# The state chain of a hybrid decoder layer with its per-head products on 128x64 tiles

## The chip, the cores and the metric

The kernel runs on one core of one Trainium2 chip. The metric is device microseconds of one execution. The core has five engines that work beside each other: PE (TensorE, the matrix engine), ACT (ScalarE), DVE (VectorE), POOL (GpSimd) and SP (SyncE, which here only issues DMAs). Each runs its own list of instructions in the order in which the program lists them and waits on semaphores for the others. A matmul reads a stationary operand, which a separate weight load (PEld in the profile) puts into the array, and a moving operand whose columns stream through it.

## The reference, cut to what matters

One layer: RMSNorm, one input projection, a pooling mixer (A) beside RWKV-7 time mixing (B), an output projection, then an MLP. The change lies in (B), in the scan over 1024 prompt tokens with 8 heads of 64:

```python
def step(S, inp):
    r_t, w_t, k_t, v_t, aa_t, bb_t = inp
    sa = jnp.einsum('bhvk,bhk->bhv', S, aa_t)
    S = S * w_t[:, :, None, :] + sa[..., None] * bb_t[:, :, None, :] + v_t[..., None] * k_t[:, :, None, :]
    return S, jnp.einsum('bhvk,bhk->bhv', S, r_t)
S_final, y = lax.scan(step, S0.astype(f32), xs)
```

## The kernel before, in words

The 1024 prompt tokens are cut into chunks of 64, and the scan is done chunk by chunk: within a chunk by matrices, from chunk to chunk by a 64x64 state per head. Heads go in pairs (`hp`, four pairs), tokens in two halves of 512, so there are eight units (`Unit`), each with 8 chunks. Partitions 0 to 63 hold head 0 of the pair, 64 to 127 head 1 (`R[0]`, `R[1]`).

For a unit, `rkv` projects r, k, v; `stage1` makes per chunk the operands `AR`, `RB`, `BKT` and `SV`; `inverse` makes `TT`, the inverse of a triangular matrix, block by block for both heads; `chain` (line 578) then runs the 8 chunks one after the other, each a step. For head h, the slice `SV[:, c, h, :]` holds the state in the head's own 64 partitions and the chunk's values in the other 64. So each product contracts over all 128 partitions. Before the change a product handles both heads at once: pq (line 601) is `AR` times `SV` for all 128 rows and both heads' 128 columns, and only the two diagonal 64x64 blocks are read on. A step is:

- `sg`: ACT scales the state (line 596)
- pq and the first part of py, the outputs (lines 601, 602): PE, stationary `AR` and `SV`
- `Q`: ACT copies pq out of PSUM (line 604)
- pa (line 605): PE, `TT` times `Q`; ACT copies its two diagonal blocks into `SV`, in place of the state (line 607)
- pu and the second part of py (lines 608, 609): PE, stationary `BKT` and `SV`
- two DVE instructions (line 617) write the new state, one per head, into the next chunk's `SV` (or into `Sf` at a unit's end)

After every four steps `ys` copies the outputs out of PSUM and `post` (line 626) normalises them. All these products are plain fp32: a 128x128 one goes through PE as two passes, each with its own weight load and its own matmul record, so the 64 executions of a line leave 128 records.

The other products of PE at that time (projections `pj`, line 185 in the helper `gemm`, the scores `sc` of line 431, transposes of lines 445 and 449, and late in the stage the output projection `mx`) are mostly 128x128 too. They stand between the chain's products. The order is not written out by hand: the parts are emitted in the sequence of `ORDER` (line 42), `chain` at a raised priority (`lead_chain`, line 824), and a scheduler that knows dependencies and its own costs lays out each engine's list when the program is built. What it lays out is fixed; at run time PE goes through its list in order. After the chain stage come the output projection, the MLP's up products (line 1014) and down products (`dn`, line 185).

Three places use smaller tiles of the array before the change: `lora_up` (line 352, 64 rows, 128 columns), the `inverse` (lines 548, 555, 565, 570: 32x32 tiles) and `decode` (line 705: 128 rows, 64 columns).

Of the kernel before, what the change touches and what calls it, by code (L numbers as in the profile page):

```python
# [7 lines left out]
F32 = mybir.dt.float32  # L8
F32R = mybir.dt.float32r
AF = mybir.ActivationFunctionType  # L10
ALU = mybir.AluOpType
# [4 lines left out]
P = 128  # L16
# [24 lines left out]
QUEUE = 1  # L41
ORDER = """R0 S0 R1 I0 S1 Q C0 R2 S2 I1 C1 R3 S3 I2 P00 P01 T I3 P02 L R4 C2 S4 C3 R5 S5 I4 R6 C4 S6 I5 R7 C5 S7 I6 C6 P10 I7 P11 P12 D"""
NBV = 3
# [43 lines left out]
def _build(ctx, nc, tc, I, O, dbg):  # L87
    V, A, PE, SY, GP = nc.vector, nc.scalar, nc.tensor, nc.sync, nc.gpsimd
# [4 lines left out]
    def act(out, in_, func=AF.Copy, bias=0.0, scale=1.0, **k):  # L93
        A.activation(out, in_, func, bias=bias, scale=scale, **k)  # L94

    def open_pool(stack, name, bufs=1, **k):
        return stack.enter_context(tc.tile_pool(name=name, bufs=bufs, **k))

    R = (slice(0, 64), slice(64, 128))
# [91 lines left out]
    rcp = open_pool(st_left, "rcp", reuse_waits="tile")  # L191
    ps_c = open_pool(st_left, "psc", 1, space=PSUM)
    pcs = ps_c.tile([P, 512], F32, name="pcs")
# [137 lines left out]
    def low_rank(half):  # L331
        n = HALF[half][1]
        z0 = big(f"z0{half}", "f")
        zw, za = (zp.tile([P, 520], F32R, tag=x, name=f"{x}{half}") for x in ("zw", "za"))
        z1 = zp.tile([P, 520], F32, tag="z1", name=f"z1{half}", bufs=2)
        shifted(12, half, z0)
        shifted(13, half, z1)
        if half:
            project_later()
        sigm(z0[0:64, :n], z0[0:64, :n], 0.0, 2.0)  # L340
        V.tensor_scalar(z0[0:64, :n], z0[0:64, :n], -2.0, 1.0, ALU.mult, ALU.add)
        for z, r, q in ((zw, R[0], R[1]), (za, R[1], R[0])):
            act(z[r, :n], z0[r, :n])
            V.tensor_tensor(z[q, :n], z0[r, :n], f32(z[r, :n]), op=ALU.subtract)
        sigm(z1[:, :n], z1[:, :n], 0.0, -1.0)
        Zt[half] = (zw, za, z1)
# [231 lines left out]
    def chain(U):  # L578
        hp = U.hp
        z1 = Zt[U.half][2]  # L580
        for i in range(2):
            nm = f"{hp}_{2 * U.half + i}"
            AR, RB, BKT, SV, TT = U.AR[i], U.RB[i], U.BKT[i], U.SV[i], U.TT
            if i == 0:
                for h in range(2):
                    if U.half == 0:
                        GP.memset(SV[R[h], 0, h, :], 0.0)
                    else:
                        act(SV[R[h], 0, h, :], Sf[hp][R[h], :])
            pyp = ps_y.tile([P, 512], F32, tag="y", name=f"py{nm}")  # L590
            py = pyp.rearrange("p (c h t) -> p c h t", h=2, t=64)
            for c in range(4):
                g = 4 * i + c
                gn = f"{U.nm}_{g}"
                sg = rcp.tile([P, 2, 64], F32, tag="sg", name=f"sg{gn}", bufs=2)
                act(sg, SV[:, c, :, :], scale=U.gam[:, g:g + 1])

                o = 256 * (hp % 2)
                pq, pa = (pcs[:, o + 128 * q:o + 128 * q + 128].rearrange("p (h t) -> p h t", t=64) for q in range(2))
                pu = pq  # L600
                PE.matmul(pq, AR[:, c, 0, :, :], SV[:, c, :, :], start=True, stop=True)  # L601
                PE.matmul(py[:, c, :, :], SV[:, c, :, :], AR[:, c, 1, :, :], start=True, stop=False)
                Q = rcp.tile([P, 2, 64], F32, tag="Q", name=f"Q{gn}", bufs=2)
                act(Q, pq)
                PE.matmul(pa, TT[:, g, :, :], Q, start=True, stop=True)  # L605
                for h in range(2):
                    act(SV[R[h], c, h, :], pa[R[h], h, :])
                PE.matmul(pu, BKT[:, c, :, :], SV[:, c, :, :], start=True, stop=True)  # L608
                PE.matmul(py[:, c, :, :], SV[:, c, :, :], RB[:, c, :, :], start=False, stop=True)
                for h in range(2):  # L610
                    if g == 7:
                        dst = Sf[hp][R[h], :]
                    elif c == 3:
                        dst = U.SV[1][R[h], 0, h, :]
                    else:
                        dst = SV[R[h], c + 1, h, :]
                    V.scalar_tensor_tensor(dst, pu[R[h], h, :], U.gam[R[h], g:g + 1], sg[R[h], h, :], ALU.mult, ALU.add)
            ys = rcp.tile([P, 256], F32, tag="ys", name=f"ys{nm}", bufs=2)
            for h in range(2):
                act(ys[R[h]].rearrange("p (c t) -> p c t", t=64), py[R[h], :, h, :])  # L620
            post(hp, nm, pyp, ys, 256, U.bv[:, 256 * i:256 * i + 256], z1[:, 256 * i:256 * i + 256], ys)
            QM.dma_start(mix_d[4 + hp][U.half][:, 256 * i:256 * i + 256], ys)
        if U.half:
            QM.dma_start(O["wkv_p"][hp], Sf[hp])

    def post(hp, nm, ps, ys, n, bv, zg, out):

        pm, pv = ps[:, 256:512], ps[:, 0:256]
        PE.matmul(pm[:, :n], CJ, ys, start=True, stop=True)
        q = rcp.tile([P, 256], F32, tag="q", name=f"q{nm}", bufs=1)  # L630
        act(q[:, :n], pm[:, :n], AF.Square)
        PE.matmul(pv[:, :n], BO, q[:, :n], start=True, stop=True)
        act(q[:, :n], pv[:, :n], AF.Ln, bias=EPSG, scale=1.0 / 64)
        act(q[:, :n], q[:, :n], AF.Exp, scale=-0.5)
        V.tensor_tensor(out, pm[:, :n], q[:, :n], op=ALU.mult)
        V.scalar_tensor_tensor(out, out, col(V_LG, hp), bv, ALU.mult, ALU.add)
        pg = pm
        PE.matmul(pg[:, :n], glu[:, hp * P:(hp + 1) * P], zg, start=True, stop=True)
        V.scalar_tensor_tensor(out, out, col(V_LB, hp), pg[:, :n], ALU.add, ALU.mult)
# [184 lines left out]
    def lead_chain(U):  # L824
        with tc.high_priority(offset=LEAD):
            chain(U)
# [18 lines left out]
    for c in ORDER.split():  # L845
# [4 lines left out]
        else:  # L850
            {"Q": pool_rows, "T": later_tokens, "L": lambda: low_rank(1), "D": decode_start}[c]()
    dec = dec[0]
# [287 lines left out]
    for b in (1, 2):  # L1140
        c, n = BLK[b]
# [88 lines left out]
```

## Time and profile before

| | |
|---|---|
| time, median of 3 runs | 1336.7 us (1336.37 to 1336.93) |
| the profiled execution's own time | 1335.81 us |
| its span, first to last instruction | 1334.0 us |
| mean granted TensorE clock | 0.991 of full speed |
| chain stage, first to last step | 67 to 521 us of the span |

PE busy is the time covered by its matmul records, whose ends are modelled and which overlap: a pass starts before the one in front has ended. So the steps from one start to the next are what a stream of passes costs, and the rows are read by starts. A row of the timeline gives the start, the length, engine, line, operation, tiles, the tile of the array (rows*columns), shapes and a count of equal instructions merged into it.

### The profile page before, as it was taken

The page shows a single profiled execution, that of the slowest core. Times are in us where ns is not written, and L with a number is a line of the kernel's source. Part 1 is how long each engine was busy: PE and PEld are TensorE (multiplying, and loading weights), DVE is VectorE, ACT ScalarE, POOL GpSimd, SP SyncE. Part 2 cuts the span into 40 slices and gives each one's busy share as a digit, 9 for nine tenths or more (in the row PEclk, how much of TensorE's full clock was granted, in tenths as well). Part 3 has the DMA queues.
Part 4 walks back from the last instruction along what each step waited for, and adds up shares of the span by engine and source line. Part 5 has one row for each costly group of instructions (what it writes and reads, how often), then busy time and mean ns, then how long its engine had stood idle before and what let it go on. Part 6 is the DMA issues. An engine that isn't in the chain of part 4 may idle for free.

```text
span 1334.0 us, 27179 instructions
## 1 busy us (share of the span) xinstructions
PE 1267.3 (95%) x10230; PEld 1146.4 (86%) x10230; DVE 1050.9 (79%) x2331; ACT 822.5 (62%) x2015; POOL 125.4 (9%) x248
## 2 busy tenths in 40 slices
PE   5999999899999989989999999999899999999996
PEld 5987788798777867789989888998799999999996
DVE  8897687778877756589989997786698787878775
ACT  7668677776777657364757564555465645455552
POOL 4101001210011021110002320001000000000000
PEclk9999999999999989999999999999899999999999
DMA  6323123222222253442335663335634323332321
GB/s 209 102 54 83 43 50 90 95 93 53 66 56 48 63 164 135 142 149 80 119 115 150 181 167 96 113 97 186 217 99 147 103 89 105 94 106 93 104 71 64
DMA packets 119492, 143.19 MB, mean 107 GB/s; under 512 B 55769, under 2 KB 71257, under 8 KB 119353
## 3 DMA queue, kind: packets, MB, share of 16 engines
q1 hardware_dynamic: 97184, 92.22, 23.7%
q0 software_dynamic: 20320, 47.39, 11.4%
q10 hardware_dynamic: 1856, 1.85, 0.4%
q8 instruction: 80, 1.31, 0.4%
q14 instruction: 52, 0.42, 0.1%
HBM read 120.68 MB, written 20.97 MB: 106 GB/s over the span
## 4 chain that ended last, share of the span: by engine, by line
PE 68%; ACT 12%; DVE 11%; DMA 5%; issue 4%; POOL 1%; SPq 0%; DVEq 0%; ACTq 0%; POOLq 0%
PE dn L185 23%; PE b L1014 21%; PE pj L185 8%; PE mx L185 4%; ACT SV L94 2%; DMA a<-in_w_up 2%; PE pcs L608 1%; PE sc L431 1%; ACT wh L94 1%; ACT TT L94 1%; PE pcs L605 1%; DVE tm L525 1%; PE pcs L601 1%; DVE wl L167 1%; PE bkt L445 1%
## 5 line engine op out<-in xcount | busy, mean ns | idle before, releaser
L185 PE MATMUL dn<-uh,wh 128*128 128x260 f32 (+1 forms) x736 | 237.7, 324 | 6.1 <-DVE x L1080 4.3
L185 PE MATMUL dn<-ul,wh 128*128 128x260 f32 (+1 forms) x736 | 237.4, 323 | 1.2 <-DVE ul L1025 1.2
L185 PE MATMUL dn<-uh,wl 128*128 128x260 f32 (+1 forms) x736 | 237.2, 323 | 1.0 <-DVE wl L167 1.0
L94 ACT ACTIVATE wh<-a 128x512 fp32r<-128x512 f32 x192 | 120.8, 629 | 161.3 <-PE dn L185 85.0
L94 ACT ACTIVATE wh<-wr 128x512 fp32r<-128x512 f32 x230 | 142.9, 622 | 98.6 <-PE dn L185 26.0
L185 PE MATMUL pj<-xh,wh 128*128 128x258 f32 (+3 forms) x576 | 172.3, 299 | 13.7 <-ACT wh L94 13.7
L167 DVE TENSOR_TENSOR wl<-wr,wh 128x512 fp32r<-128x512 f32 x230 | 155.7, 681 | 35.4 <-ACT wh L94 27.5
L185 PE MATMUL pj<-xl,wh 128*128 128x258 f32 (+3 forms) x576 | 170.3, 296 | 0.0
L185 PE MATMUL pj<-xh,wl 128*128 128x258 f32 (+3 forms) x576 | 170.0, 295 | 0.1
L185 PEld LDWEIGHTS dn<-uh,wh 128*128 128x128 f32 x736 | 138.9, 189 | 17.3 <-ACT uh L94 3.2
L185 PEld LDWEIGHTS dn<-uh,wl 128*128 128x128 f32 x736 | 138.8, 189 | 12.3 <-DVE wl L167 1.2
L185 PEld LDWEIGHTS dn<-ul,wh 128*128 128x128 f32 x736 | 138.9, 189 | 10.8 <-DVE ul L1025 1.8
L176 DVE TENSOR_TENSOR wl<-a,wh 128x512 fp32r<-128x512 f32 x192 | 131.3, 684 | 6.2 <-ACT wh L94 3.6
L1080 DVE TENSOR_TENSOR x<-dn,x 128x260 f32<-128x260 f32 (+1 forms) x192 | 97.6, 511 | 41.5 <-PE dn L185 39.9
L185 PEld LDWEIGHTS pj<-xh,wh 128*128 128x128 f32 x576 | 109.9, 191 | 17.6 <-ACT wh L94 13.7
L185 PEld LDWEIGHTS pj<-xl,wh 128*128 128x128 f32 x576 | 110.0, 191 | 2.3 <-issue 1.9
L185 PEld LDWEIGHTS pj<-xh,wl 128*128 128x128 f32 x576 | 109.8, 191 | 1.8 <-issue 1.0
L94 ACT ACTIVATE c<-c 128x256 f32<-128x256 f32 (+1 forms) x128 | 53.1, 415 | 45.7 <-DVE c L1029 45.2
L991 DVE TENSOR_TENSOR a<-a,a 128x512 f32<-128x512 f32 x96 | 66.2, 689 | 19.0 <-DMA a<-in_w_up 17.5
L1025 DVE TENSOR_TENSOR ul<-u,uh 128x256 fp32r<-128x256 f32 (+1 forms) x128 | 53.6, 423 | 18.8 <-ACT uh L94 18.4
L185 PE MATMUL mx<-mh,wh 128*128 128x260 f32 (+1 forms) x192 | 64.9, 341 | 3.3 <-ACT mh L94 1.9
L185 PE MATMUL mx<-ml,wh 128*128 128x260 f32 (+1 forms) x192 | 63.6, 332 | 0.9 <-DVE ml L881 0.9
(421 smaller groups left out, 3388.6 us busy)
## 6 DMA issues: line engine op xcount, KB each, us to landing
a<-in_w_up SPq DMA_DIRECT2D x128, 256.0 KB, 2.6
wr<-in_w_down SPq DMA_DIRECT2D x128, 256.0 KB, 2.6
wr<-in_w_in POOLq DMA_DIRECT2D x72, 256.0 KB, 3.1
wr<-in_w_out POOLq DMA_DIRECT2D x26, 256.0 KB, 3.2
xr<-in_xT SPq DMA_DIRECT2D x16, 256.0 KB, 3.6
mr<-mix SPq DMA_DIRECT2D x8, 260.0 KB, 4.3
x<-in_xT SPq DMA_DIRECT2D x4, 520.0 KB, 5.0
blk<-AA SPq DMA_DIRECT2D x16, 128.0 KB, 2.7
```

Of the source, the lines that this page charges most:

```text
L94: A.activation(out, in_, func, bias=bias, scale=scale, **k)
L167: V.tensor_tensor(l[:, :w], raw[:, :w], f32(h[:, :w]), op=ALU.subtract)
L176: V.tensor_tensor(l, raw, f32(h), op=ALU.subtract)
L185: PE.matmul(ps, lhs, rhs, start=i == 0, stop=i == n - 1)
L431: PE.matmul(psc[:, c, :], BK[:, c, 2 * h:2 * h + 2, :], AR[:, c, :, h, :], start=True, stop=True)
L445: PE.transpose(pt[:, c, :], BK[:, c, 2 * h:2 * h + 2, :].rearrange("p a t -> p (a t)"), ident)
L525: V.tensor_tensor(pr[:, q], l[:, q].unsqueeze(2).to_broadcast([64, m, m, m]), r[:, q].rearrange("p k j -> p j k").unsqueeze(1).to_broadcas ...
L601: PE.matmul(pq, AR[:, c, 0, :, :], SV[:, c, :, :], start=True, stop=True)
L991: V.tensor_tensor(a[out], a[x], a[y], op=op)
L1014: PE.matmul(ps, lhs[:, c], rhs, start=k == i == 0, stop=k == 3 and i == 2)
L1025: V.tensor_tensor(ul, u, f32(uh), op=ALU.subtract)
L1080: V.tensor_tensor(d, ps[:, :n], d, op=ALU.add)
```

## The change

The two heads' products are issued one by one. Each keeps the contraction over 128 partitions, but loads 64 columns of weights and moves 64 columns, on the half of the array's columns that belongs to the head (tile position 0 or 64), so that its result lands in the head's 64 partitions of PSUM. Only the diagonal blocks are computed. pq, pa, pu, `Q` and `ys` become compact: 64 columns instead of 2x64. `pa` stays one product with the block-diagonal `TT` on the whole array, with 64 moved columns. pu gets its own place in PSUM instead of pq's. `ys` is one ACT copy instead of two.

```diff
--- before.py
+++ after.py
@@ -588,7 +588,7 @@
                     else:
                         act(SV[R[h], 0, h, :], Sf[hp][R[h], :])
             pyp = ps_y.tile([P, 512], F32, tag="y", name=f"py{nm}")
-            py = pyp.rearrange("p (c h t) -> p c h t", h=2, t=64)
+            py = pyp[:, 0:256].rearrange("p (c t) -> p c t", t=64)
             for c in range(4):
                 g = 4 * i + c
                 gn = f"{U.nm}_{g}"
@@ -596,17 +596,20 @@
                 act(sg, SV[:, c, :, :], scale=U.gam[:, g:g + 1])
 
                 o = 256 * (hp % 2)
-                pq, pa = (pcs[:, o + 128 * q:o + 128 * q + 128].rearrange("p (h t) -> p h t", t=64) for q in range(2))
-                pu = pq
-                PE.matmul(pq, AR[:, c, 0, :, :], SV[:, c, :, :], start=True, stop=True)
-                PE.matmul(py[:, c, :, :], SV[:, c, :, :], AR[:, c, 1, :, :], start=True, stop=False)
-                Q = rcp.tile([P, 2, 64], F32, tag="Q", name=f"Q{gn}", bufs=2)
+                pq, pa, pu = (pcs[:, o + 64 * q:o + 64 * q + 64] for q in range(3))
+                for h in range(2):
+                    PE.matmul(pq[R[h]], AR[:, c, 0, h, :], SV[:, c, h, :], start=True, stop=True)
+                for h in range(2):
+                    PE.matmul(py[R[h], c, :], SV[:, c, h, :], AR[:, c, 1, h, :], start=True, stop=False)
+                Q = rcp.tile([P, 64], F32, tag="Q", name=f"Q{gn}", bufs=2)
                 act(Q, pq)
                 PE.matmul(pa, TT[:, g, :, :], Q, start=True, stop=True)
                 for h in range(2):
-                    act(SV[R[h], c, h, :], pa[R[h], h, :])
-                PE.matmul(pu, BKT[:, c, :, :], SV[:, c, :, :], start=True, stop=True)
-                PE.matmul(py[:, c, :, :], SV[:, c, :, :], RB[:, c, :, :], start=False, stop=True)
+                    act(SV[R[h], c, h, :], pa[R[h]])
+                for h in range(2):
+                    PE.matmul(pu[R[h]], BKT[:, c, h, :], SV[:, c, h, :], start=True, stop=True)
+                for h in range(2):
+                    PE.matmul(py[R[h], c, :], SV[:, c, h, :], RB[:, c, h, :], start=False, stop=True)
                 for h in range(2):
                     if g == 7:
                         dst = Sf[hp][R[h], :]
@@ -614,10 +617,9 @@
                         dst = U.SV[1][R[h], 0, h, :]
                     else:
                         dst = SV[R[h], c + 1, h, :]
-                    V.scalar_tensor_tensor(dst, pu[R[h], h, :], U.gam[R[h], g:g + 1], sg[R[h], h, :], ALU.mult, ALU.add)
+                    V.scalar_tensor_tensor(dst, pu[R[h]], U.gam[R[h], g:g + 1], sg[R[h], h, :], ALU.mult, ALU.add)
             ys = rcp.tile([P, 256], F32, tag="ys", name=f"ys{nm}", bufs=2)
-            for h in range(2):
-                act(ys[R[h]].rearrange("p (c t) -> p c t", t=64), py[R[h], :, h, :])
+            act(ys, pyp[:, 0:256])
             post(hp, nm, pyp, ys, 256, U.bv[:, 256 * i:256 * i + 256], z1[:, 256 * i:256 * i + 256], ys)
             QM.dma_start(mix_d[4 + hp][U.half][:, 256 * i:256 * i + 256], ys)
         if U.half:
```

On PE, the list of the program before at the second and third step of a unit (`sc`, `bkt`, `vt`, `pj` belong to other units; L608 and L609 end a step, L601 and L602 begin the next, L605 is pa):

```order
L608 MATMUL pcs<-SV_0_1223,BKT_0_1222 128x128
L609 MATMUL py_0_1922<-RB_143,SV_0_1223 128x128
L445 MATMUL bkt_0_1_1716<-cst,BK 128x128 x4
L449 MATMUL vt_0_1722<-cst,v_0_1433 128x128 x2
L601 MATMUL pcs<-SV_0_1223,AR_139 128x128
L602 MATMUL py_0_1922<-AR_139,SV_0_1223 128x128
L185 MATMUL pj_1_2170<-xh_205,wh 128x258
L185 MATMUL pj_1_2170<-xl_206,wh 128x258
L605 MATMUL pcs<-Q_0_1_1940,TT_158 128x128
```

The same unit in the changed program, from the end of its second step to the third's pa (L610 is pu, L612 and L603 are py, L601 is pq, L606 is pa; 64x64 is one head's product):

```order
L610 MATMUL pcs<-SV_0_1223,BKT_0_1222 64x64 x2
L612 MATMUL py_0_1952<-RB_143,SV_0_1223 64x64 x2
L431 MATMUL sc_1_1_1775<-AR_138,BK 128x128
L185 MATMUL pj_0_2271<-xh_171,wl 128x256
...
L445 MATMUL bkt_1_0_1785<-cst,BK 128x128 x2
L603 MATMUL py_0_1952<-AR_139,SV_0_1223 64x64
L445 MATMUL bkt_1_0_1785<-cst,BK 128x128 x2
L601 MATMUL pcs<-SV_0_1223,AR_139 64x64 x2
L603 MATMUL py_0_1952<-AR_139,SV_0_1223 64x64
L185 MATMUL pj_0_2271<-xh_171,wl 128x256
```

The first head's py product now stands by itself among whole-array products, ahead of the two pq products: it needs only the first of the two DVE instructions that write the state.

And the end of the fourth step of that unit in the changed program, PE again:

```order
L606 MATMUL pcs<-Q_0_3_2010,TT_158 128x64
L185 MATMUL pj_1_2300<-xl_206,wh 128x258
L185 MATMUL pj_1_2300<-xh_205,wl 128x258
L185 MATMUL pj_1_2300<-xh_205,wh 128x258
L612 MATMUL py_0_1952<-RB_143,SV_0_1223 64x64
L610 MATMUL pcs<-SV_0_1223,BKT_0_1222 64x64 x2
L612 MATMUL py_0_1952<-RB_143,SV_0_1223 64x64
L185 MATMUL pj_1_2300<-xl_206,wh 128x258
```

Here one head's second py product moved ahead of the two pu products, and the four stand together. Over the whole list the chain's 64x64 products form 184 separate groups with whole-array or other tiles between them; 53 of them begin with L603 (45 of these hold that one product alone), 59 with L601, 72 with L610 or L612. The list before has none.

## Rows read from the trace of the kernel before

**Rows 1.** The page: busy time of PE; its share in 40 slices; engines of the last chain.

```profile
PE 1267.3 (95%) x10230; PEld 1146.4 (86%) x10230; DVE 1050.9 (79%) x2331; ACT 822.5 (62%) x2015; POOL 125.4 (9%) x248
PE   5999999899999989989999999999899999999996
PE 68%; ACT 12%; DVE 11%; DMA 5%; issue 4%; POOL 1%; SPq 0%; DVEq 0%; ACTq 0%; POOLq 0%
```

**Rows 2.** Windows: the chain stage (length, then busy us per engine, clock, DMA).

```profile
67.00:521.00 454.00, 426.75 (x4225) 362.29 (x4224) 343.74 (x847) 327.13 (x930) 55.17 (x112) 0.99 0.28 77
```

**Rows 3.** Lines 601 and 608: matmul records, ns min/median/max, first and last start.

```profile
L601 PE MATMUL pcs<-SV,AR x128: 270/275/378, 67.5 to 517.9; 128*128 128x128 f32 x128
L608 PE MATMUL pcs<-SV,BKT x128: 270/275/421, 107.2 to 520.2; 128*128 128x128 f32 x128
```

**Rows 4.** Waits of PE, 67 to 521 us: us in total, times, longest us.

```profile
PE pcs L601 <- DVE SV L617: 3.3, 8, 1.0
PE pcs L608 <- ACT SV L94: 3.2, 11, 0.5
```

**Rows 5.** Waits of PE's weight loads, same stretch.

```profile
PEld pcs L608 <- ACT SV L94: 18.3, 50, 0.7
PEld pcs L601 <- DVE SV L617: 6.7, 16, 1.2
```

**Rows 6.** Timeline, weight loads of the end of a step.

```profile
113.49 0.30 PEld L608 LDWEIGHTS pcs<-SV,BKT 128*128 128x128 f32 x2 [0.39 <-ACT SV L94]
113.71 0.30 PEld L609 LDWEIGHTS py<-RB,SV 128*128 128x128 f32 x2
```

**Rows 7.** Timeline around line 705, the 128*64 tiles before the change.

```profile
523.20 0.69 DVE L703 TENSOR_TENSOR dS<-dS,dW 128x512 f32<-128x512 f32 x1
523.76 0.39 PE L185 MATMUL mx<-mh,wl 128*128 128x512 f32 x1
524.00 0.40 PE L185 MATMUL mx<-mh,wh 128*128 128x512 f32 x1
524.32 1.01 PEld L705 LDWEIGHTS dpa<-r,dS 128*64 128x64 f32 x16 [0.37 <-DVE dS L703]
525.35 0.19 PEld L185 LDWEIGHTS mx<-ml,wh 128*128 128x128 f32 x1
525.45 0.19 PEld L185 LDWEIGHTS mx<-mh,wl 128*128 128x128 f32 x1
```

**Rows 8.** Line 705's weight loads: ns min/median/max.

```profile
L705 PEld LDWEIGHTS dpa<-r,dS x64: 132/138/138, 512.9 to 543.6; 128*64 128x64 f32 x64
```

**Rows 9.** Timeline around line 570: two 32*32 tiles, in rows and columns apart.

```profile
143.79 0.58 PEld L570 LDWEIGHTS pi<-TX,Z 32*32 32x32 f32 x32 [0.38 <-ACT Z L94]
144.42 0.19 PEld L185 LDWEIGHTS pj<-xh,wl 128*128 128x128 f32 x1
144.52 0.19 PEld L185 LDWEIGHTS pj<-xh,wh 128*128 128x128 f32 x1
```

**Rows 10.** Line 570's weight loads.

```profile
L570 PEld LDWEIGHTS pi<-TX,Z x256: 101/108/108, 104.0 to 486.5; 32*32 32x32 f32 x128
```

**Rows 11.** Timeline ahead of a group of line 548.

```profile
134.76 0.28 PE L185 MATMUL pj<-xl,wh 128*128 128x256 f32 x1
134.88 0.28 PE L185 MATMUL pj<-xh,wl 128*128 128x256 f32 x1
134.99 0.28 PE L185 MATMUL pj<-xh,wh 128*128 128x256 f32 x1
135.20 0.21 PEld L548 LDWEIGHTS pi<-TX,AA 16*32 16x32 f32 x15
```

**Rows 12.** ACT by form, 67 to 521 us (count, busy us, mean ns, idle before).

```profile
L94 ACT ACTIVATE SV<-pcs 64x64 f32<-64x64 f32 x128 | 27.6, 216 | 12.9 <-PE pcs L605 11.4
L94 ACT ACTIVATE Q<-pcs 128x128 f32<-128x128 f32 x64 | 17.6, 275 | 4.0 <-PE pcs L601 2.1
L94 ACT ACTIVATE ys<-py 64x256 f32<-64x256 f32 x31 | 11.7, 377 | 4.0 <-PE py L609 3.4
```

## The prediction

> **What bounds the kernel now.** I read the page first: PE is busy 95% of the span, nine tenths or more in nearly every slice, and carries 68% of the last chain; ACT and DVE have room [rows 1]. Then the windows: the change touches 67 to 521 us alone, and there PE is busy 426.75 of 454 us at a clock of 0.99 [rows 2]. Since PE works through a fixed list, time added to that list moves everything behind it, except where it falls into a wait. Next the chain's lines: each of the five products of a step leaves 128 records for 64 steps, so two passes each [rows 3]. Then the waits, to see how much PE stands still for the chain: 3.3 us at pq for the state and 3.2 us at pu for `SV` [rows 4]. The weight loads wait longer, 18.3 us in 50 waits at pu and 6.7 us in 16 at pq [rows 5], but part of that lies under matmuls that still stream. So the chain's results are late only a little, and what counts is how much of PE's list the chain takes.
>
> What it takes is read by starts. The two loads of line 608 begin at 113.49 and those of line 609 at 113.71 [rows 6]: two passes in 0.22 us, 0.110 us each, though one record is 270 ns long [rows 3]. A load of 128 columns sets that step. A step of the scan has 10 such passes, 1.10 us; 64 steps take 70.4 us, of which pa, which stays on the whole array, has 14.1 us and the four other products 256 x 2 x 0.110 = 56.3 us.
>
> **The change part by part.** Four whole-array products of a step become eight of half the width: 512 products, 1024 passes, each with a load of 64 columns. The only 128*64 tiles before are line 705's: 16 loads from 524.32 in 1.01 us, the last 0.138 long, so 15 steps in 0.872 us, 0.058 us a pass [rows 7, 8]. These 16 all write the same half of the array's columns. Were the chain's passes to follow each other like them, they would take 1024 x 0.058 = 59.4 us: 3.1 us more than now. That is one end.
>
> The other end is that the two halves run side by side. No row of before has two tiles that differ in columns alone. The nearest in which two tiles alternate is line 570, whose two differ in rows and columns: 32 loads in 0.58 us, the last 0.108 long, so 31 steps in 0.472 us, 0.015 us a pass [rows 9, 10]. A 32-column load by itself would be some 0.03 us, half of line 705's 0.058, so two of them run in the time of one. Counting in each group of the list the half with more products, 310 of the 512 remain in sequence (a lone product has no partner, and two pq with one py make two): 620 x 0.058 = 36.0 us, 20.3 us less than now.
>
> I take this end: it is the row in which two tiles alternate at all, and line 705, which never leaves its half, can't show an overlap. That both halves read the same rows is what could undo it, and the other end stays in the range.
>
> Of the pages, two speak to this and differ. The Trainium skill, TensorEngine Tiling (Array Packing), Key Properties, says that tiles work independently, loads and matmuls in parallel; by it the sum is the second end. The Trainium skill, TensorE: Matmul & The Clock Gate, The mechanism, says that a load overlaps matmuls in flight only where the row group differs, and the chain's two halves have the same rows. For two passes on the whole array the trace disagrees with that: the load at 113.71 begins while a 270 ns matmul of line 608 runs [rows 3, 6]. For two halves no run here shows it.
>
> **What the tiles' change itself costs.** This is the larger part. Into the smaller tiles: passes of line 185 start 0.115 us apart (134.76, 134.88, 134.99), so the next pass would start at 135.11; but the load for line 548's smaller tiles begins at 135.20, not under the pass in front but after it [rows 11]. With 0.058 us for a 64-column load the first pass starts at 135.26, 0.15 us late. Line 705 says the same: passes of 512 columns start 0.24 apart, the next would start at 524.23 or 524.24, the load begins at 524.32 and the first pass 0.058 later, at 524.38. That is no wait for data, since what it is said to wait for, `dS`, was done at 523.89 [rows 7]. Out again: line 705's last load starts at 524.32 + 0.87 = 525.19, the next in a stream would start at 525.25, and the one for the whole array starts at 525.35, 0.10 late [rows 7]; after line 570 it is 143.79 + 0.47 = 144.26, then 144.42 instead of some 144.29, 0.13 late [rows 9]. Line 705 moves 2 columns a pass, the chain 64, so I take 0.13.
>
> The changed list goes into such tiles and out of them 184 times, where the list before stays on whole tiles for the chain. The ways in are free where the load waits for data anyway, with an empty array: 50 waits at pu and 16 at pq [rows 5]. The other 118 cost 118 x 0.15 = 17.7 us. The ways out, 184 x 0.13 = 23.9 us. A part falls into the 6.5 us in which PE stands still at pq and pu [rows 4]; I take off half, 3 us.
>
> **The rest.** pa keeps its two 128-column loads: nothing. ACT: `Q` goes from 275 ns to about the 216 ns of a 64-column copy, 64 x 0.059 = 3.8 us; `ys` from two copies of 377 ns to one, 16 x 0.377 = 6.0 us [rows 12]. ACT is busy 327 of 454 us [rows 2], so I cost these at nothing; the waits that would show them are those of PE above. DVE keeps its two instructions a step. No DMA is added, and no wait on another engine: a head's product waits for that head's half, earlier than both did. What is behind a waiting product on PE are the other units' projections, the same as before.
>
> Sum: -20.3 + 17.7 + 23.9 - 3 = +18.3 us. The span of 1334.0 becomes 1352.3, the profiled execution's 1335.8 becomes 1354.1, and since the median of the runs shown is 0.9 above that execution, the prediction is 1355.
>
> **The rivals.**
>
> 1. The two halves don't overlap: the passes cost +3.1 instead of -20.3, the sum is +41.7, 1378 us. For it: same rows for both, and line 705's steady 0.058. Against: rows 9. This is also the case in which the change does not do what its name says. By the rule on row groups of the Trainium skill, TensorE: Matmul & The Clock Gate, The mechanism, it would be this one.
> 2. As 1, and neither the ways in nor PE's standstill hide anything, because the lone py product puts a way out and another way in just ahead of pq, which the scheduler did not price: 184 x 0.15 + 23.9 + 3.1 = 54.6, 1391 us.
> 3. Faster: the chain's own length decides, not PE's list. Every way in or out then falls into a wait, and a step loses 0.06 at `Q`, 0.11 since the first head's state update starts a pass pair earlier, and 0.09 for its share of `ys`: 0.26 x 64 = 16.6 us, 1320 us. For it: 50 of 64 pu loads wait for ACT [rows 5]. Against: PE stands still only 6.5 us at those places and 27 us in the whole stage [rows 2, 4], while 42 us of changes of tile have to be hidden; it decides only from the point where these waits exceed what is added.
> 4. No change: the forecast's overlap, with most of the 27 us of standstill swallowing its 21 us; 1337 us. Against: those waits lie largely elsewhere than at the chain's products.
>
> **How the numbers follow.** The forecast has 0.50, rival 1 0.30, rival 2 0.06, rival 3 0.10, rival 4 0.04. The forecast's own range, with the price of a change of tile a quarter off either way, is 1345 to 1366. A measurement of this kernel can't tell less than 0.2% (2.7 us) from no change. Faster than that: rival 3 and a little of 4, 0.11; within it: 0.04; slower: 0.85. For eight in ten I leave out rival 3 and most of 4 below, and rival 2 above: 1338 to 1386.
>
> **What the profile of the changed kernel would show.** Overlap: in a group with both heads, loads of the two heads a few ns apart and pairs 0.058 apart; without it, loads 0.058 apart throughout. The change of tile: the load of a group's first product begins some 0.09 us later than the pass step would have it, and the first 128*128 load behind a group some 0.13 late; the page's PE share stays near 95% while the chain stage ends 18 us later (42 without overlap), and the stage from there to the end keeps its 813 us. The forecast is wrong if the stage's end moves by less than 5 us, or if the groups' ways in are as short as a pass, or if waits at pq, pa and pu grow by more than the changes of tile cost.

## The result, and the profile after

The changed kernel takes 1346.85 us, median of 4 runs (1342.89 to 1347.93), against 1336.82 (4 runs) before: a ratio of 1.0069 (of the means), 95% interval 1.0049 to 1.009, so 9.2 us more; the medians lie 10.0 apart. It is slower, inside the range and at about half of the forecast 18.3 us. The profiled execution took 1342.89 us, with a span of 1341.0 us.

The page of the changed kernel: engines, PE's slices, engines of the last chain.

```profile
PE 1283.0 (96%) x10742; PEld 1145.5 (85%) x10742; DVE 1050.4 (78%) x2331; ACT 813.7 (61%) x1999; POOL 125.0 (9%) x248
PE   5999998999999989989999999999899999999996
PE 70%; DVE 9%; ACT 8%; issue 6%; DMA 4%; POOL 2%; DVEq 0%; POOLq 0%; SPq 0%; ACTq 0%
```

PE has 512 more records and is a little busier than in [rows 1]; ACT does 16 instructions fewer. The windows of the changed kernel, the chain stage to its last step and what is behind it:

```profile
67.00:537.50 470.50, 451.62 (x4789) 366.81 (x4787) 348.92 (x856) 324.70 (x936) 56.49 (x115) 0.99 0.28 78
537.50:1341.00 803.50, 778.09 (x5563) 728.68 (x5563) 646.15 (x1338) 441.03 (x967) 48.36 (x90) 0.99 0.39 120
```

The stage ends 16.5 us later than in [rows 2], but what follows is 9.5 us shorter than the 813 us of before: PE now has 53 more records of other work ahead of the last chain product (4027 instead of 3974, counted in the traces), which are then missing behind it. So the stage's end alone does not give the difference.

The halves overlap. Weight loads of the changed kernel at the end of a step, where the two heads' pu and py stand together:

```profile
111.10 0.20 PEld L610 LDWEIGHTS pcs<-SV,BKT 128*64 128x64 f32 x4 [0.33 <-ACT SV L94]
111.21 0.20 PEld L612 LDWEIGHTS py<-RB,SV 128*64 128x64 f32 x4
```

The four loads of pu start within 0.11 us and those of py follow at once: eight passes in 0.23 us, where four whole-tile passes took 0.44 [rows 6]. In the 19 groups of this form the loads start by the medians 0.007 us apart within a pair and 0.055 to 0.059 from pair to pair.

The changes of tile. PE in the changed kernel, a lone py product and the next step's pq, with other units' whole tiles around them:

```profile
116.35 0.28 PE L185 MATMUL pj<-xl,wh 128*128 128x256 f32 x1
116.56 0.33 PE L603 MATMUL py<-AR,SV 128*64 128x64 f32 x2
116.82 0.38 PE L185 MATMUL pj<-xh,wl 128*128 128x256 f32 x1
117.13 0.34 PE L601 MATMUL pcs<-SV,AR 128*64 128x64 f32 x4
117.31 0.28 PE L603 MATMUL py<-AR,SV 128*64 128x64 f32 x2
117.52 0.38 PE L185 MATMUL pj<-xh,wh 128*128 128x256 f32 x1
```

By their ends, the passes of line 185 in front of and behind the lone product are 116.63 and 117.20: 0.57 us apart instead of 0.115. The lone product thus costs 0.455 us, of which its two passes are 0.116 and the ways in and out 0.34. The 49 lone products between whole tiles cost 0.462 us by the median, in the measure of the ledger below; six groups of two pq products, which use both halves, cost 0.474. So a change of tile is paid by the group, and the second head's product beside the first adds only 0.012. The ways in and out are those of [rows 11] and [rows 7], now in 184 groups. The weight loads at the same place:

```profile
116.24 0.19 PEld L185 LDWEIGHTS pj<-xl,wh 128*128 128x128 f32 x1
116.56 0.19 PEld L603 LDWEIGHTS py<-AR,SV 128*64 128x64 f32 x2
116.82 0.19 PEld L185 LDWEIGHTS pj<-xh,wl 128*128 128x128 f32 x1
```

The second of the two merged loads starts at 116.61.

The waits. Weight loads of the changed kernel that wait for the chain, 67 to 538 us:

```profile
PEld pcs L610 <- ACT SV L94: 4.3, 13, 0.8
PEld py L612 <- ACT SV L94: 3.3, 11, 0.5
PEld py L603 <- DVE SV L620: 2.8, 7, 0.8
```

At pu and the py beside it 7.6 us are left of the 18.3 in [rows 5], at pq and its py some 3 of the 6.7. The copies of ACT in the changed kernel, by form:

```profile
L94 ACT ACTIVATE Q<-pcs 128x64 f32<-128x64 f32 x64 | 14.2, 221 | 18.5 <-PE pcs L601 17.7 <-PE py L603 0.4
L94 ACT ACTIVATE ys<-py 128x256 f32<-128x256 f32 x16 | 6.1, 384 | 2.0 <-PE py L612 1.7
```

`Q` went from 275 to 221 ns and `ys` from two copies of 377 to one of 384 [rows 12], as priced; but ACT now stands idle 18.5 us ahead of `Q` instead of 4.0. It waits for a PE that comes late.

**A ledger of PE's list.** PE hardly stops, so its span can be split. For every group of chain products (pq, py, pa, pu) I took the time from the end of the last other record in front to the end of the first behind, less the step such a record has in a stream (0.110 us up to 250 columns, 0.113 at 256, 0.219 at 512). The sum is what the chain takes of PE, waits included. "Passes" are 0.110 us each on whole tiles and 0.058 per pair on halves, "changes" 0.34 us a group of half tiles, "rest" is what remains: waits, and the part of a load that no matmul in front hides. Only the first and the last column are measured; the three between split the first by counts and these prices. The last column is all other records of PE.

| kernel | chain's share of PE, us | passes | changes | rest | other records |
|---|---|---|---|---|---|
| before | 121.7 | 70.4 | 0 | 51.3 | 1188.6 |
| before, second profile | 122.8 | 70.4 | 0 | 52.4 | 1190.7 |
| changed | 129.3 | 50.1 | 62.6 | 16.6 | 1188.2 |
| changed, second profile | 129.7 | 50.1 | 62.6 | 17.0 | 1189.7 |
| py grouped | 108.5 | 44.1 | 44.2 | 20.2 | 1198.3 |
| whole tiles, 64 moved | 100.2 | 70.4 | 0 | 29.8 | 1194.3 |
| py twice, whole tiles | 137.2 | 84.5 | 0 | 52.7 | 1199.1 |
| lone half tile added | 135.2 | 77.8 | 21.8 | 35.6 | 1199.4 |
| only py compact, whole tiles | 112.4 | 70.4 | 0 | 42.0 | 1188.6 |
| only the path compact, whole tiles | 110.8 | 70.4 | 0 | 40.4 | 1192.3 |

The 7.6 us between the first and the third row are the 7.0 us between the spans. In the four rows from "py grouped" to "lone half tile added" the other records take 4 to 9 us more than in the second profile of before, so there the ledger's difference is not the whole difference in time. These four ran on another chip, from which there is no profile of before. The 5053 records from the MLP's first product to the end, where nothing was changed, are 1.1 to 2.4 us of it (719.7 us in the second profile of before, 720.8 to 722.1 in the four); what the rest is stays open.

### The profile page after: what moved, and what is told of

Same layout as the page of the kernel before. It is cut to its first block, busy times and chain, and to the rows that moved or that the text cites. A ratio compares the mean times of both kernels' runs of the same rounds, so it can differ in the third digit from the quotient of the medians.

```text
span 1341.0 us, 28235 instructions
## 1 busy us (share of the span) xinstructions
PE 1283.0 (96%) x10742; PEld 1145.5 (85%) x10742; DVE 1050.4 (78%) x2331; ACT 813.7 (61%) x1999; POOL 125.0 (9%) x248
## 4 chain that ended last, share of the span: by engine, by line
PE 70%; DVE 9%; ACT 8%; issue 6%; DMA 4%; POOL 2%; DVEq 0%; POOLq 0%; SPq 0%; ACTq 0%
PE dn L185 20%; PE b L1016 16%; PE pj L185 14%; PE mx L185 5%; PE sc L431 2%; DMA a<-in_w_up 1%; PE py L603 1%; PE py L612 1%; PE bkt L445 1%; PE pcs L601 1%; ACT TT L94 1%; ACT wh L94 1%; PE pcs L610 1%; DVE wl L167 1%; DVE x L1088 1%
## 5 line engine op out<-in xcount | busy, mean ns | idle before, releaser
L185 PE MATMUL pj<-xh,wh 128*128 128x258 f32 (+3 forms) x576 | 175.0, 304 | 13.5 <-ACT wh L94 13.5
L185 PE MATMUL pj<-xh,wl 128*128 128x258 f32 (+3 forms) x576 | 173.2, 301 | 0.1
L185 PEld LDWEIGHTS dn<-uh,wh 128*128 128x128 f32 x736 | 138.9, 189 | 18.3 <-ACT uh L94 4.2
L185 PEld LDWEIGHTS pj<-xh,wh 128*128 128x128 f32 x576 | 109.8, 191 | 19.7 <-ACT wh L94 13.5
L1027 DVE TENSOR_TENSOR ul<-u,uh 128x256 fp32r<-128x256 f32 (+1 forms) x128 | 53.9, 425 | 18.9 <-ACT uh L94 18.4
```

The lines of the kernel that those rows point to most:

```text
L185: PE.matmul(ps, lhs, rhs, start=i == 0, stop=i == n - 1)
L1027: V.tensor_tensor(ul, u, f32(uh), op=ALU.subtract)
```

## The experiments

Each ratio is to runs of the kernel before on the same chip: one chip (1338.53 us, median of 17) for py grouped, all compact on whole tiles, py twice and the lone half tile, another (1336.85, of 12) for the others.

**The py products queued behind pq and pu.** Theory: the changes of tile are the cost. Rival: the lone products fill waits.

```diff
                 for h in range(2):
-                    PE.matmul(pq[R[h]], AR[:, c, 0, h, :], SV[:, c, h, :], start=True, stop=True)
-                for h in range(2):
-                    PE.matmul(py[R[h], c, :], SV[:, c, h, :], AR[:, c, 1, h, :], start=True, stop=False)
+                    m = PE.matmul(pq[R[h]], AR[:, c, 0, h, :], SV[:, c, h, :], start=True, stop=True)
+                with tc.issue_after(m.ins):
+                    for h in range(2):
+                        PE.matmul(py[R[h], c, :], SV[:, c, h, :], AR[:, c, 1, h, :], start=True, stop=False)
...
```

(The same for pu and the second part of py.)

> The changed kernel with one thing altered: the two py products of a step are queued behind the two pq products (and behind the two pu products), so that no product stands by itself. The list then has 130 groups of half tiles instead of 184. My theory: in the changed kernel's trace the 43 lone py products took 20.1 us of PE's list and 8 lone second parts 3.7 us, nearly all of it for going into and out of the half tiles; without them PE's list is some 23 us shorter, of which waits for the state and for Q take back up to half: 1326 to 1336 us, against 1346.9 for the changed kernel. Rival: a lone product only fills time in which PE would have waited for the second head's state, so the time stays at 1344 to 1348 us.

Measured: 1332.26 us, ratio 0.9946 (0.9927 to 0.9965). That is 0.54% below before, and 1.2% (16 us) below the changed kernel by the two ratios. The rival falls. In the ledger, 54 groups fewer save 18.4 us of changes and 6.0 of passes, since only three products are left without a partner; waits take 3.6 back. That is 20.8 us by the profiles, whose spans are only 10.4 us apart, since the other records take 10.1 more; by the ratios the gain is 16. Weight loads of this kernel around one step:

```profile
117.12 0.19 PEld L185 LDWEIGHTS pj<-xl,wh 128*128 128x128 f32 x1
117.45 0.20 PEld L611 LDWEIGHTS pcs<-SV,BKT 128*64 128x64 f32 x4
117.56 0.20 PEld L614 LDWEIGHTS py<-RB,SV 128*64 128x64 f32 x4
117.83 0.19 PEld L185 LDWEIGHTS pj<-xh,wl 128*128 128x128 f32 x1
```

Nearly every step has two such groups and no third (130 groups in 64 steps). This version beats both kernels.

**The same compact products on whole tiles.** It takes the change of tile and the overlap away and keeps the rest. Half of each result is left out, so it measures and is no version to use; the same holds for the next two.

```diff
-                for h in range(2):
-                    PE.matmul(pq[R[h]], AR[:, c, 0, h, :], SV[:, c, h, :], start=True, stop=True)
+                PE.matmul(e2(pq), AR[:, c, 0, :, :], SV[:, c, :, 0:32], start=True, stop=True)
...
```

(py and pu likewise; `e2` views 64 columns as two heads of 32.)

> The changed kernel's compact results and its ACT copies, but its products on whole 128x128 tiles with 64 moved columns, so that no tile is changed and no halves overlap. (Each product moves the first 32 columns of each head alone, so the other half of its results is left out.) My theory: PE's list holds the passes of the kernel before at 0.110 us each, and the time is that of before or a little below, since Q and ys are shorter: 1330 to 1338 us. Rival: what made the changed kernel slower is the compact layout and the order that the scheduler makes of it, not the tiles: 1344 to 1348 us.

Measured: 1318.27 us, ratio 0.9844 (0.9824 to 0.9864): 20.9 us below before. The rival falls, but my theory missed too: it expected the time of before, since the passes are the same. The loads of pu and py start 0.109 to 0.112 us apart by the medians, in this kernel as in before, so the passes cost the same though they move half the columns. The gain is in the rest, 51.3 to 29.8. Waits of this kernel's weight loads:

```profile
PEld pcs L608 <- ACT SV L94: 11.4, 41, 0.8
PEld pcs L601 <- DVE SV L617: 2.0, 5, 0.7
PEld pcs L605 <- ACT Q L94: 1.8, 5, 0.6
```

So compactness, which I had costed at nothing, is worth some 21 us here. The next two runs ask how.

**Only py compact, and only the path compact.**

```diff
-                PE.matmul(py[:, c, :, :], SV[:, c, :, :], AR[:, c, 1, :, :], start=True, stop=False)
+                PE.matmul(py[:, c, :, :], SV[:, c, :, :], AR[:, c, 1, :, 0:32], start=True, stop=False)
...
```

> The kernel before with only its two py products and ys compact: whole tiles, 64 moved columns (the first 32 of each head; the rest of py's results is left out). pq, pa, pu and Q stay wide. py is off the path from one state to the next. Theory A (the earlier run with all products compact on whole tiles gained because the path pq, Q, pa, pu got shorter): nothing of that here, 1333 to 1339 us where before has 1337 to 1339. Theory B (it gained because the scheduler, pricing narrow products lower, puts more of other units' passes into each wait; its list here has 5.5 such passes between pq and pa and 5.8 between pa and pu where before has 4.6 and 4.8): 1318 to 1327 us.

```diff
-                PE.matmul(pq, AR[:, c, 0, :, :], SV[:, c, :, :], start=True, stop=True)
+                PE.matmul(e2(pq), AR[:, c, 0, :, :], SV[:, c, :, 0:32], start=True, stop=True)
...
```

> The other part: pq, pa, pu and Q compact on whole tiles with 64 moved columns (the first 32 of each head; the rest of pq's and pu's results is left out), py and ys wide as before. Theory A (a shorter path): 1317 to 1324 us, nearly all of the gain. Theory B (more passes in the waits; this list has 4.1 between pq and pa and 5.6 between pa and pu): 1330 to 1337 us.

Measured: 1326.11 us, ratio 0.9918 (0.9894 to 0.9941), and 1328.8 us, ratio 0.9941 (0.992 to 0.9962): 11 and 8 us below before. The first lies in theory B's range, the second between the ranges of A and B, so neither theory holds alone. Against the second profile of before, the ledger gives -10.4 and -12.0, together about the -22.6 of all compact. With py alone compact, the waits for `Q` shrink, as the first fence (second profile of before) and the second (only py compact) show, though the path is as long as before:

```profile
PEld pcs L608 <- ACT SV L94: 19.0, 50, 1.1
PEld pcs L605 <- ACT Q L94: 6.9, 25, 0.4
```

```profile
PEld pcs L608 <- ACT SV L94: 17.0, 49, 0.8
PEld pcs L605 <- ACT Q L94: 3.1, 10, 0.8
```

With the path compact it is the other wait that shrinks:

```profile
PEld pcs L608 <- ACT SV L94: 10.5, 33, 0.9
PEld pcs L605 <- ACT Q L94: 7.7, 22, 1.0
```

This fits a mixture: a shorter path, and a list in which the scheduler puts more of other units' passes into a wait (by the median step, 4 records of other work between pq and pa with py compact, 3 before and 2 with the path compact, counted in the traces, where the expectations' averages are higher). That the passes in the list are the cause in the first case follows from its unchanged path only by exclusion; a run with the same list and wide products was not made.

**The first py product twice, on whole tiles.**

```diff
+                PE.matmul(py[:, c, :, :], SV[:, c, :, :], AR[:, c, 1, :, :], start=True, stop=True)
                 PE.matmul(py[:, c, :, :], SV[:, c, :, :], AR[:, c, 1, :, :], start=True, stop=False)
```

> The kernel before with the first py product of each step issued twice, on whole tiles: 64 x 2 passes x 0.110 = 14.1 us more in PE's list, off the chain's own path. This measures how much of an addition to PE's list the chain's waits swallow. My theory: about half, +5 to +9 us, 1342 to 1346 us. Rival a: PE's list is all that counts, +14 us, 1351. Rival b: the waits swallow it, within 2 us of before.

Measured: 1359.6 us, ratio 1.0152 (1.0132 to 1.0173): +20.3 us. My theory missed; even rival a, all 14.1 us, is too low. In the ledger the passes' 14.1 us are there in full and the waits are as before (52.7). The order has a reason: with the second copy 1 record of other work stands between pq and pa by the median step instead of 3, so the copy stands where filling work stood, and the wait stays. The remaining 5 us are not in the chain's groups; all other records take 1199.1 us in this profile, 1190.7 in the second of before, on another chip. What they are stays open.

**A lone product on a half tile added to the kernel before.**

```diff
+                PE.matmul(py[R[0], c, 0, :], SV[:, c, 0, :], AR[:, c, 1, 0, :], start=True, stop=True)
                 PE.matmul(pq, AR[:, c, 0, :, :], SV[:, c, :, :], start=True, stop=True)
```

> The kernel before with one product of 64 columns on a half tile added per step, on the first head's operands, by itself among whole-tile products: 64 more groups of two passes, as the changed kernel's lone py products. Its two passes alone are 64 x 2 x 0.058 = 7.4 us; with the way into and out of the half tile the changed kernel's trace has 0.468 us a group, 30.0 us. My theory: about half of that stays, +12 to +18 us, 1349 to 1355 us. Rival a: changes of tile fall into waits and only the passes count: +3 to +7 us, 1340 to 1344. Rival b: all of it counts: 1367 us.

Measured: 1358.68 us, ratio 1.0137 (1.0113 to 1.0161): +18.3 us (15.1 to 21.5), just past the upper end of my theory's +12 to +18; rivals a and b fall. PE in this kernel:

```profile
111.54 0.28 PE L185 MATMUL pj<-xh,wl 128*128 128x258 f32 x1
111.75 0.33 PE L601 MATMUL py<-AR,SV 128*64 128x64 f32 x2
112.01 0.39 PE L185 MATMUL pj<-xh,wh 128*128 128x258 f32 x1
```

By ends 111.82 to 112.40, 0.58 us for two short passes and one usual step, as in the changed kernel. In the ledger 29.2 us are added and 15.7 of them come out of the waits; that leaves 13.5 of the 18.3, and the rest is not in the chain's groups. Two passes of 64 columns on a half tile so cost about as much as two passes of 128 on whole tiles in the run before, and 21.8 of the 29.2 us are the change of tile.

**The changed kernel again, and the kernel before again.**

> The changed kernel again, on the chip of these runs: 0.4 to 1.0% above before, 1344 to 1351 us, as all theories have it. It gives the comparison with the run in which its py products are grouped on equal terms: if that run's gain was a matter of the chip, this one will be near 1338.

> The kernel before again, for a profile from the same chip as the experiments: 1336 to 1343 us; PE's list outside the chain's products within 1% of 1189 us, and 120 to 125 us in the chain's groups.

Measured: 1345.41 us, ratio 1.0066 (1.0044 to 1.0089), and 1339.06 us in its one run. Both as expected. The grouped version and the changed kernel were not timed on one chip, so the 16 us between them rest on the two ratios: 0.54% below before on the one, 0.66% above it on the other.

## Why the prediction was right, and where it was off

- The overlap held, step and size: pairs of passes 0.055 to 0.058 us apart, by which the passes are at -20.3 us, and two pq products on both halves cost hardly more than one product alone (0.474 and 0.462 us a group). Rival 1, no overlap, is out. So is, for two halves of columns, the rule on row groups of the Trainium skill, TensorE: Matmul & The Clock Gate, The mechanism: in the group at 111.10 four loads on both halves start within 0.11 us, while the first matmul, 0.27 us long, still runs, though their rows of the array are the same. That section also lets a load run ahead into a background weight buffer, a case that the prediction left out when it set the rule against the whole-array trace. What the Trainium skill says in TensorEngine Tiling (Array Packing), Key Properties, of tiles that run side by side agrees with the trace: 0.058 us for a pair.
- The ways in and out were mis-sized: 0.15 and 0.13 in the prediction, 0.28 together; measured 0.34. The way in was right: the load at 116.56 is 0.09 behind the step, as forecast. On the way out the load is 0.15 late instead of 0.13 (116.61 + 0.058 is 116.67, and it starts at 116.82). I had not counted that this whole-tile load then sets a step of 0.110 us where the count went on with 0.058, some 0.05 more. 184 groups cost 62.6 us instead of 51.5.
- The waits were mis-sized the other way, and by more. The prediction let 66 free ways in (9.9 us) and 3 us of standstill swallow 12.9 us. The step that failed is the one that took PE's 6.5 us [rows 4] for what there was to swallow: in the chain's groups there were 51.3 us beyond the passes, since a wait whose start lies under the modelled end of a record is not counted as idle, and a record of 0.27 us stands for a pass of 0.110. Of these 51.3 us 34.7 are gone.
- "I cost these at nothing" failed for `Q`, and I had no line at all for the shorter products. By medians over the 64 steps, from the first load to the last record's end, pq and pu went from 0.490 to 0.337 us each, pa from 0.490 to 0.449, `Q` from 0.278 to 0.223: 0.40 us of a step. From pq's first load to the written state a step takes 3.60 us before and 3.14 after, waits included. On whole tiles compactness alone gave 20.9 us. That was rival 3's mechanism; it is real, but the changes of tile outweighed it. In the ledger the rest falls by 21.5 us in that run already, which would leave 13.2 of the 34.7 for what was swallowed, near the forecast 12.9. The lists of the two kernels differ, so how the 34.7 us divide between these two steps is not shown.
- So the forecast's sum -20.3 + 51.5 - 12.9 = 18.3 became, by the ledger, -20.3 + 62.6 - 34.7 = 7.6. Sign and mechanism were right, with two terms off by 11 and 22 us in opposite directions. That the sign held is in part luck: with the forecast's own price of a change and the waits as they turned out, the sum is -3.5. The stage's end moved by 16.5 us, close to the 18 named, but the stage behind it did not keep its 813 us.
- The lone py product was named in the order and in rival 2; without it and its like the change is no longer slower. With the py products grouped, the same idea is 7.2 us faster than before.

## What to carry to other kernels

Count the groups, not the products: a visit to another tile shape costs 0.34 us here however little is in it, so products on part of the array have to stand together in PE's list, and a scheduler that starts each as soon as its operand is ready takes them apart. Size the waits that an edit can use up from the steps between starts and ends around a group, not from an idle column. And price what gets shorter on the way from one state to the next even where its engine has room: on whole tiles, with no pass saved, it gave 20.9 us, as much as the overlap was to save.

## What was not expected of the hardware

Two fp32 products on the two halves of the array's columns run pass by pass in turn, though the list has one product ahead of the other: the four loads of two pu products start in two close pairs, 0.055 us from pair to pair, in the group at 111.10, and where the list has py, pu, pu, py (ten groups), the records start as py, pu, py, pu, pu, py, pu, py. And a pass of 64 moved columns on whole tiles is no cheaper in a stream than one of 128: in both kernels the loads of pu and py start 0.109 to 0.112 us apart; what it gives is an earlier result, pq's end at 0.447 instead of 0.490 us after its first load. These ends are modelled; from pq's first load to the written state the median step takes 3.22 us there and 3.60 before, waits included.
